# A two-layer diffusion trunk on one core: weight tiles of the modulation vectors loaded one step ahead of their dots, a fifth raw tile, and wider steps for the first layer's S5 tables

## The chip, the cores and the metric

One Trainium2 chip, one core. The metric is the device time of one execution in microseconds. The kernel before took 1841.99 us (median of 3 runs, 1840.18 to 1842.88).

## The reference, cut to what matters

The trunk has two layers over 256 latent tokens and 256 context tokens of width 1024 (512 columns in all). A layer is a SwiGLU half-step, a mixing sub-layer (windowed attention, a bidirectional S5 state-space part and a short gated convolution) and a second SwiGLU half-step. Each of the three sub-layers normalizes its input, shifts and scales it, and gates its output, with nine modulation vectors per layer that are products of a conditioning vector with a 1024 x 9216 matrix:

```python
def _modulate(x, g, shift, scale):
    return _rms_norm(x, g) * (1 + scale) + shift

def _gated_post(y, g, gate):
    return gate * _rms_norm(y, g)

def _swiglu(h, wg, wu, wd):
    return (jax.nn.silu(h @ wg) * (h @ wu)) @ wd

def _ffn_sublayer(x, m, s, g_pre, g_post, wg, wu, wd):
    h = _modulate(x, g_pre, m[:, 3 * s], m[:, 3 * s + 1])
    return _gated_post(_swiglu(h, wg, wu, wd), g_post, m[:, 3 * s + 2])
```

All is float32. The vectors are made for two conditioning inputs (latent and context tokens), so each weight tile of them is read by two dots.

## The kernel before, in words

**Products.** A float32 weight tile of 128 x 1024 comes from DRAM into a *raw* tile `wr` (`wraw`, L122), is rounded to `wh` by ACT (L131), and the rest `wl` is taken by POOL or DVE (L134). Activations are split the same way into `xh` (ACT, L608) and `xl` (DVE, L609), and a product is three matmuls, `wh` with the high part, `wh` with the low part and `wl` with the high part (`mm3`, L146; the matmuls are on L156). There are four raw tiles. They serve every such weight, the weights of the modulation vectors and a few scratch tiles of the S5 part.

**Stages.** FFN(0,0) is the first half-step of layer 0, then come the mixer of layer 0, FFN(0,1), FFN(1,0), the mixer of layer 1 and the last half-step. A half-step has 22 blocks of 128 hidden columns in four groups of 5, 5, 5 and 7: for each block the gate and up products (`pgu`), then the gate (`g`, ACT L606) times up (L607 on DVE, in place in `pgu`) and its split (L608, L609); after a group the down products (`pd`), which go through its blocks for one part of the output after the other, so that the first part needs all five blocks; L655 adds it into `y`. A half-step's first two column spans are run at 256 columns (`sk`), because the norm of the sub-layer ahead is still being formed for the second span.

**The boundary between sub-layers** (`boundary`, L372). For each of eight parts `d`, DVE makes `ss` (L381) and adds it into the stream `x` (L383); ACT squares it, PE sums the columns (`ss`, L341), DVE forms 1/sqrt in some ten small operations (L295 to L325) and puts it on a diagonal `dg` (L329), PE spreads it over the partitions (`rb`, L334), and DVE and ACT make the normalized input (`hh`, `hl`, L364 to L367).

**Side work.** Two kinds of side work run as generators beside the products: `ada` (L272) forms one modulation vector from eight tiles of 128 x 1024 of `w_ada`, each with two dots on DVE (L249; only one for the last vectors of layer 1); `ssm_tables` (L838) forms the S5 part's tables for a layer. A generator yields a number of ticks, and `mm3` counts ticks per matmul (1 tick is 2370 columns of matmul). When enough have passed, the generator's next piece is written into the program. So the tables `DTA` (per half-step, 5.1, 7.0 and 6.64 ticks per tile of `w_ada`) and `YS` (per piece of the S5 tables) say where in PE's order the pieces stand. The order of PE is fixed by this. The orders of DVE, ACT, POOL and SP come from a scheduler that works with its own times, and raw tiles are given to whichever load comes next in that order.

**The S5 tables of layer 0** are made in FFN(0,0) in four quarters. In a quarter POOL forms `tx` and `tvv` (L904, L907), PE transposes `tx` (`wt`, L914) after `YS[l][4]` ticks, twice, and after `YS[l][5]` makes `kp` (L934), which DVE finishes (`tz`, L939). `wt` and `kp` share two PSUM tiles. After the fourth quarter POOL makes the rotations (L956 to L978), and only behind those stand its `wl` splits for the last group's down weights.

**Queues.** SP issues every load and waits in order: a load that waits for its raw tile holds up those behind it, the loads `ts` of the S5 tables (L853 to L856) among them.

Of the kernel before, what the change touches and what calls it, by code (L numbers as in the profile page):

```python
# [8 lines left out]
F32 = mybir.dt.float32  # L9
# [12 lines left out]
KD = 8  # L22
# [8 lines left out]
FGROUPS = (tuple(range(0, 5)), tuple(range(5, 10)), tuple(range(10, 15)), tuple(range(15, 22)))  # L31
RF = -27.0 / 1024
MAGIC_ROUND = 12582912.0
RAW = 4
WB = 6
FIRST = 3
SKEW_IN = 4
# [31 lines left out]
DTA = (5.1, 7.0, 6.64)  # L69
YB = (2.2, 2.43, 9.63)  # L70
YP = (45.0, 8.0, 4.12, 5.43, 8.37, 8.88, 12.75)
YS = ((6.42, 1.34, 4.28, 18.82, 6.31, 3.09, 0.29, 3.43, 7.65), (6.0, 2.0, 4.0, 16.0, 16.0, 4.0, 2.0, 4.0, 8.0))
YA = (1.0, 5.0, 0.1)
ND = 3
NDL = 2
# [3 lines left out]
class Trunk:  # L79
# [42 lines left out]
    def wraw(self, src, cols=1024):  # L122
        w = self.wpool.tile([128, 1024], F32, name=self.nm("wr"), tag="wr", bufs=RAW)
        self.nc.sync.dma_start(w[:, :cols], src)
        return w
# [147 lines left out]
    def ada(self, l, m, dt):  # L273
        first = 1 if l == NL - 1 and m >= 5 else 0
        if first:
            self.nc.gpsimd.memset(self.mod[l][:, m], 0.0)
        for b in range(KD):
            w = self.wraw(self.a["w_ada"][l, m, b])
            for s in range(first, 2):
                self.ada_dot(w, l, m, b, s)  # L280
            yield dt
        self.ada_end(l, m, slice(0, KD))
        yield 0.1

# [121 lines left out]
    def rows(self):  # L406

        nc = self.nc
        l = NL - 1
        for i in range(2):  # L410
            p = self.pm("pr")
            nc.tensor.matmul(p[:KD, :128], self.pv[l][i + 1][:, :, 1], self.ident, start=True, stop=True)
            t = self.slots.tile([128, 512], F32, name=self.nm("bt"), tag="bt", bufs=2)[:KD, :128]
            nc.scalar.activation(t, p[:KD, :128], AF.Copy)
            dr = self.dram.tile([KD, 128], F32, name=self.nm("pvr"))
            nc.sync.dma_start(dr, t)
            nc.sync.dma_start(self.sb[:, i], dr.rearrange("d p -> (d p)")[None, :].to_broadcast([128, D]))
            yield

        self.xr = []  # L420
        for t in range(2):
            self.xr.append([])
            for h in range(2):
                p = self.pm("pxr")
                for d in range(4):
                    c = CTX + t * 128
                    nc.tensor.transpose(p[:, d * 128:d * 128 + 128], self.x[4 * h + d][:, c:c + 128], self.ident)
                d = 4 * t + 2 * h
                x = self.xall[:, d:d + 2, :256]
                p = p.rearrange("p (a b) -> p a b", a=2)  # L430
                if h:
                    nc.vector.tensor_copy(x, p)
                else:
                    nc.scalar.activation(x, p, AF.Copy)
                self.xr[t].append(x)
                yield
# [296 lines left out]
    def ssm_params(self):  # L733
# [25 lines left out]

        pw = self.wpool.tile([128, 1024], F32, name=self.nm("pw"), tag="wr", bufs=RAW)[:, :2 * 9 * w]  # L760
        pw = pw.rearrange("p (i k w) -> p i k w", i=2, k=9)
# [76 lines left out]
    def ssm_tables(self, l):  # L838
# [19 lines left out]
        par = [self.gg[:, :, l * 16:l * 16 + 16], self.u8[:, :, l * 16:l * 16 + 16], self.m8[:, l * 16:l * 16 + 16]]  # L858
        yield YS[l][0]
        b, c, pws, pr = tb("tvv", 2), tb("tc"), tb("tpw"), self.tpr  # L860
        for s_, d_ in zip(src, (b, c, pws)):
# [5 lines left out]
            else:  # L867
                nc.scalar.activation(d_, p, AF.Copy)
            yield YS[l][1]
        p = self.pm("tp")  # L870
        for s_, o, n in zip(par, (0, 32, 64), (32, 32, 16)):
            nc.tensor.matmul(p[:, o:o + n], self.ident, s_, start=o == 0, stop=True, skip_group_check=True)
        nc.scalar.activation(pr, p[:, :80], AF.Copy)
        yield YS[l][2]
        gg_, u8_ = (pr[:, o:o + 32].rearrange("p (i g) -> p i g", i=2) for o in (0, 32))
# [10 lines left out]
        for i, (x, y, o) in enumerate(((0, 1, OP.subtract), (1, 0, OP.add))):  # L886
# [3 lines left out]
            g.tensor_tensor(bbv[i][:, :, :16], tv[:, 0], tv[:, 1], op=o)  # L890
        yield YS[l][3]
        zd = self.dram.tile([256, 240], F32, name=self.nm("Z"))
        for gq in range(4):
# [3 lines left out]
            for ri in range(2):  # L897
# [12 lines left out]
                VV.append(vv)  # L910
                yield YS[l][4]
                pt = self.pm("wt")
# [6 lines left out]
                nc.sync.dma_start(self.V[l, gq // 2, ri][:, o], vv)  # L919
            yield YS[l][5]  # L920
            kp = self.pm("kp"), self.ps("kp")
# [63 lines left out]
    def ssm_chunks1(self, u):  # L985
# [3 lines left out]
        for half in range(2):  # L989
            t = self.wpool.tile([128, 1024], F32, name=self.nm("ut"), tag="wr", bufs=RAW)  # L990
            for jh in range(2):
# [77 lines left out]
    def ssm_out(self, l, gh, U, S, lo):  # L1069
# [6 lines left out]
        vt = [self.wraw(self.V[l, gh, ri]) for ri in range(2)]  # L1076
        yt = self.wpool.tile([128, 1024], F32, name=self.nm("yt"), tag="wr", bufs=RAW)
        ng, r = 128 // n, 8 * n // 128
# [139 lines left out]
    def mixer(self, l, H, pend, newH):  # L1218
# [143 lines left out]
        def early_out(n):  # L1362
# [10 lines left out]
            v=lambda n: vtok(), k=lambda n: ksplit(), q=qsplit,  # L1373
            s=lambda n: S.append(self.ssm_states(l, n, U)), o=lambda n: yt.append(self.ssm_out(l, n, U, S[n], lo)),
            b=lambda n: G.append(self.ssm_back(yt[n], lo)), w=weight, r=lambda n: next(rows, None),
            g=lambda n: self.ssm_glu(l, G, cat, lo), e=early_out, x=tail if last else bound, S=attn_s,
            y=lambda n: oevac(n // 10, n % 10), z=lambda n: self.advance(out[0][1]), W=weight,
# [19 lines left out]
    def first(self, H, ws):  # L1397
# [9 lines left out]
        nc.scalar.activation(self.cv, self.cv, AF.Silu)  # L1407
        nc.vector.tensor_copy(cv[:, :, :2], self.cv)
        rows, xn = {}, {}

        def row(d, *ms):
# [211 lines left out]
```

## Time and profile before

| | |
|---|---|
| median of 3 runs | 1841.99 us |
| profiled execution | 1845.4 us, span of the core 1843.1 us, 2.3 us around it |
| mean granted clock of TensorE | 0.968 |
| PE busy | 1724.7 us (94%) |
| DVE busy | 1139.7 us (62%) |
| POOL busy | 711.7 us (39%) |
| ACT busy | 657.8 us (36%) |

Busy time of PE counts a slow matmul as busy, so its share says little of how much is lost; what is lost shows as idle time ahead of a matmul and as a granted clock of 0.5, at which a matmul takes twice as long. A bracket behind an instruction is the idle time of its engine just before it, and what ended it.

### The profile page before, as it was taken

To read this page: it belongs to the slowest core of one execution; us is meant where nothing else is said; L and a number is where in the kernel's file an instruction comes from. 1 tells how busy PE (TensorE), PEld (TensorE's weight loads), DVE (VectorE), ACT (ScalarE), POOL (GpSimd) and SP (SyncE) were. 2 spreads that over 40 slices of the span, in tenths; PEclk is the share of its full clock that TensorE was granted. 3 is DMA by queue.
4 is the path that set the end of the run, shared out by engine and by line. 5 is a ranking of instruction groups with operands and counts; after the bars stand their busy time and mean duration, and the time that the engine had idled before them with its cause. 6 is when DMAs were issued, how large, how long until landed. Compare 5 with 4: busy or idle time off the path is not lost.

```text
span 1843.1 us, 28602 instructions
## 1 busy us (share of the span) xinstructions
PE 1724.7 (94%) x11040; PEld 1483.2 (80%) x11040; DVE 1139.7 (62%) x2228; ACT 657.8 (36%) x1173; POOL 711.7 (39%) x623
## 2 busy tenths in 40 slices
PE   7999988998987989999999989999999899889998
PEld 5887876898975879887888989888888897679997
DVE  5798786726479655787774265765456466852223
ACT  4332222324334543322222243322222344445443
POOL 4100886854344142563438343000001553435552
PEclk9999998999999988999999999999999989899999
DMA  7666556644144021665655331646466424445662
GB/s 279 227 221 179 183 175 185 212 137 127 35 143 142 26 82 43 197 193 180 194 189 166 96 115 55 227 147 200 126 205 221 128 93 140 145 151 174 191 184 92
DMA packets 103481, 285.94 MB, mean 155 GB/s; under 512 B 19904, under 2 KB 27152, under 8 KB 103344
## 3 DMA queue, kind: packets, MB, share of 16 engines
q1 hardware_dynamic: 102992, 283.91, 49.1%
q8 instruction: 87, 1.43, 0.3%
q14 instruction: 50, 0.41, 0.1%
q0 software_dynamic: 64, 0.12, 0.0%
q10 hardware_dynamic: 288, 0.07, 0.0%
HBM read 270.45 MB, written 15.70 MB: 155 GB/s over the span
## 4 chain that ended last, share of the span: by engine, by line
PE 71%; DVE 13%; DMA 6%; issue 4%; POOL 3%; ACT 3%; SPq 0%; DVEq 0%; ACTq 0%; POOLq 0%
PE pgu L156 32%; PE pd L156 17%; PE sk L156 8%; PE yr L484 4%; DMA wr<-in_w_ada_dram 3%; DVE junk L249 3%; PE po L156 2%; DVE wl L134 2%; PE ss L341 1%; ACT wh L131 1%; DMA wr<-in_w_in_dram 1%; PE pgu L535 1%; PE O L1209 1%; DVE xacc L354 1%; DVE ss L381 1%
## 5 line engine op out<-in xcount | busy, mean ns | idle before, releaser
L134 POOL TENSOR_TENSOR wl<-wr,wh 128x1024 fp32r<-128x1024 f32 (+1 forms) x140 | 326.1, 2345 | 704.7 <-ACT wh L131 314.1
L131 ACT ACTIVATE wh<-wr 128x1024 fp32r<-128x1024 f32 (+2 forms) x350 | 341.8, 983 | 636.3 <-PE pgu L156 164.9
L156 PE MATMUL pgu<-hh,wh 128*128 128x512 f32 (+1 forms) x1296 | 469.8, 363 | 0.0
L156 PE MATMUL pgu<-hl,wh 128*128 128x512 f32 (+1 forms) x1296 | 465.2, 359 | 0.0
L156 PE MATMUL pgu<-hh,wl 128*128 128x512 f32 (+1 forms) x1296 | 465.2, 359 | 0.0
L249 DVE SCALAR_TENSOR_TENSOR junk<-wr,sb 128x1024 bf16<-128x1024 f32 x224 | 311.9, 1392 | 164.9 <-DMA wr<-in_w_ada_dram 163.2
L134 DVE TENSOR_TENSOR wl<-wr,wh 128x1024 fp32r<-128x1024 f32 (+1 forms) x210 | 251.4, 1199 | 70.0 <-ACT wh L131 69.2
L156 PEld LDWEIGHTS pgu<-hh,wh 128*128 128x128 f32 x1296 | 244.6, 189 | 41.1 <-issue 1.7
L156 PEld LDWEIGHTS pgu<-hl,wh 128*128 128x128 f32 x1296 | 244.6, 189 | 39.8 <-issue 0.5
L156 PEld LDWEIGHTS pgu<-hh,wl 128*128 128x128 f32 x1296 | 244.3, 189 | 39.2
L156 PE MATMUL pd<-xh,wh 128*128 128x512 f32 (+1 forms) x696 | 245.6, 353 | 7.6 <-ACT xh L608 7.6
L156 PE MATMUL pd<-xl,wh 128*128 128x512 f32 (+1 forms) x696 | 241.6, 347 | 1.1 <-DVE xl L609 1.1
L156 PE MATMUL pd<-xh,wl 128*128 128x512 f32 (+1 forms) x696 | 240.6, 346 | 0.0
L156 PEld LDWEIGHTS pd<-xh,wh 128*128 128x128 f32 x696 | 135.0, 194 | 25.9 <-ACT xh L608 8.9
L156 PEld LDWEIGHTS pd<-xl,wh 128*128 128x128 f32 x696 | 134.8, 194 | 19.6 <-DVE xl L609 2.8
L156 PEld LDWEIGHTS pd<-xh,wl 128*128 128x128 f32 x696 | 134.7, 194 | 16.2
L156 PE MATMUL sk<-hh,wh 128*128 128x256 f32 x480 | 141.6, 295 | 0.0
L156 PE MATMUL sk<-hl,wh 128*128 128x256 f32 x480 | 139.1, 290 | 0.1
L156 PE MATMUL sk<-hh,wl 128*128 128x256 f32 x480 | 138.8, 289 | 0.0
L608 ACT ACTIVATE xh<-pgu 128x512 fp32r<-128x512 f32 (+1 forms) x61 | 35.0, 574 | 175.5 <-DVE pgu L607 175.3
L156 PEld LDWEIGHTS sk<-hl,wh 128*128 128x128 f32 x480 | 94.7, 197 | 0.6 <-DVE hl L367 0.3
L156 PEld LDWEIGHTS sk<-hh,wh 128*128 128x128 f32 x480 | 94.7, 197 | 0.3
(375 smaller groups left out, 2479.4 us busy)
## 6 DMA issues: line engine op xcount, KB each, us to landing
wr<-in_wgu_dram SPq DMA_DIRECT2D x170, 512.0 KB, 4.3
wr<-in_w_ada_dram SPq DMA_DIRECT2D x144, 512.0 KB, 4.3
wr<-in_wd_dram SPq DMA_DIRECT2D x72, 320.0 KB, 3.2
wr<-in_w_in_dram SPq DMA_DIRECT2D x32, 512.0 KB, 3.9
wr<-in_wd_dram SPq DMA_DIRECT2D x36, 448.0 KB, 3.8
wr<-in_wdr_dram SPq DMA_DIRECT2D x22, 512.0 KB, 3.6
wr<-in_w_out_dram SPq DMA_DIRECT2D x10, 512.0 KB, 5.0
V<-tvv SPq DMA_DIRECT2D x16, 256.0 KB, 2.8
```

Of the source, the lines that this page charges most:

```text
L131: nc.scalar.activation(h[:, :cols], w[:, :cols], AF.Copy)
L134: eng.tensor_tensor(lo[:, :cols], w[:, :cols], h.bitcast(F32)[:, :cols], op=OP.subtract)
L156: mm = lambda a_, x_, st, sp: nc.tensor.matmul(po, a_[:, c], x_[:, lo:hi], start=st, stop=sp, skip_group_check=True)
L249: self.nc.vector.scalar_tensor_tensor(self.junk, w, 1.0, self.sb[:, s], op0=OP.mult, op1=OP.mult, accum_out=self.mod[l][:, m, b, s:s + 1])
L341: self.nc.tensor.matmul(p[:, b:b + 1], t[:, lo + b * 128:lo + (b + 1) * 128], self.ones[:, 0:1], start=first and b == 0, stop=last, skip_g ...
L354: nc.vector.tensor_tensor(acc[:, lo:hi], acc[:, lo:hi], sq, op=OP.add)
L381: nc.vector.scalar_tensor_tensor(bt, y[d][:, lo:hi], self.pv[l][s_][:, d, s:s + 1], rb[:, :hi - lo], op0=OP.mult, op1=OP.mult)
L484: mm = lambda x_, a_, st, sp: self.nc.tensor.matmul(p, x_[:, c], a_[:, o:o + 512], start=st, stop=sp, skip_group_check=True)
L535: nc.tensor.matmul(ps[i // 2][:, o:o + 128], w[:, k * 128:k * 128 + 128], U[k][:, t * 128:t * 128 + 128], start=t + n + i % 2 == 0, stop=n ...
L608: nc.scalar.activation(gh[:, lo:hi], pu, AF.Copy)
L1209: nc.tensor.matmul(O[pr, :w], vt[:, kt * 128 + 64 * ab:kt * 128 + 64 * ab + 64], PT[ab][:, kt * w:(kt + 1) * w], start=kt == 0, stop=kt == ...
```

## The change

There are five edits. A fifth raw tile (`RAW`). In `ada`, the load of tile b + 1 is written one step before the dots of that tile, so that a load has a whole step (5.1 to 7.0 ticks) before its dots; the loads stand at the same ticks as before and the dots one step later. In the first layer's S5 tables, `YS[0][4]` goes from 6.31 to 8.3 and `YS[0][5]` from 3.09 to 4.0, so that a quarter takes 2 x 8.3 + 4.0 + 0.29 = 20.89 ticks in place of 16.00. In `rows`, two small tiles move to the common pool of 39, which frees the room for the fifth raw tile. All lines behind L280 stand five lines lower in the changed kernel.

```diff
-RAW = 4
+RAW = 5
-YS = ((6.42, 1.34, 4.28, 18.82, 6.31, 3.09, 0.29, 3.43, 7.65), (6.0, 2.0, 4.0, 16.0, 16.0, 4.0, 2.0, 4.0, 8.0))
+YS = ((6.42, 1.34, 4.28, 18.82, 8.3, 4.0, 0.29, 3.43, 7.65), (6.0, 2.0, 4.0, 16.0, 16.0, 4.0, 2.0, 4.0, 8.0))
...
+        load = lambda b: self.wraw(self.a["w_ada"][l, m, b])
+        ws = [load(0)]
+        yield dt
         for b in range(KD):
-            w = self.wraw(self.a["w_ada"][l, m, b])
+            if b < KD - 1:
+                ws.append(load(b + 1))
             for s in range(first, 2):
-                self.ada_dot(w, l, m, b, s)
-            yield dt
+                self.ada_dot(ws[b], l, m, b, s)
+            if b < KD - 1:
+                yield dt
         self.ada_end(l, m, slice(0, KD))
         yield 0.1
...
-            t = self.slots.tile([128, 512], F32, name=self.nm("bt"), tag="bt", bufs=2)[:KD, :128]
+            t = self.slot("pvt")[:KD, :128]
```

**How the order moves, 1: DVE at the boundary ahead of FFN(0,1).** These are the last of the eight parts and the start of the 1/sqrt. Before:

```order
L381 SCALAR_TENSOR_TENSOR ss_6766<-y_4810,pv_105,rb_6818 128x256
L383 TENSOR_TENSOR x<-x,ss_6766 128x256
L607 TENSOR_TENSOR sk_6743<-g_6905,sk_6743 128x256
L295 TENSOR_SCALAR v_6974<-ss_6969 128x2
L609 TENSOR_TENSOR xl_6904<-sk_6743,xh_6903 128x256
```

In the changed kernel, with the rest of the 1/sqrt:

```order
L386 SCALAR_TENSOR_TENSOR ss_6766<-y_4810,pv_105,rb_6818 128x256
L249 SCALAR_TENSOR_TENSOR junk,mod_96<-wr_7352,sb 128x1024
L388 TENSOR_TENSOR x<-x,ss_6766 128x256
L249 SCALAR_TENSOR_TENSOR junk,mod_96<-wr_7352,sb 128x1024
L612 TENSOR_TENSOR sk_6743<-g_6905,sk_6743 128x256
L300 TENSOR_SCALAR v_6974<-ss_6969 128x2
```

```order
L330 TENSOR_SCALAR r_6980<-rd_6983,ri_6976 128x1 x2
L249 SCALAR_TENSOR_TENSOR junk,mod_96<-wr_7416,sb 128x1024
L323 TENSOR_SCALAR t_6988<-r_6980,v_6974 128x1 x2
L249 SCALAR_TENSOR_TENSOR junk,mod_96<-wr_7416,sb 128x1024
L330 TENSOR_SCALAR r_6989<-t_6988,r_6980 128x1 x2
L334 TENSOR_SCALAR dg_6994<-ident,r_6989 128x128 x2
```

The four dots of the first two tiles of this half-step, which stood behind all of the boundary's work, now stand inside its chain. The same four stand at the same places of the chain ahead of FFN(1,0).

**How the order moves, 2: SP at the same place.** The loads from the last gate and up weights ahead of FFN(0,1)'s first tile of `w_ada` on; the name behind "waits" is the engine whose reading frees the raw tile. In the changed kernel:

```order
L124 DMA wr_7341<-in_wgu_dram 128x1024 [waits DMAHW0_49,Pool_49]
L124 DMA wr_7352<-in_w_ada_dram 128x1024 [waits DMAHW1_49,Pool_49]
L124 DMA wr_7416<-in_w_ada_dram 128x1024 [waits DMAHW6_49,DVE_49]
L124 DMA wr_7451<-in_wd_dram 128x640 [waits DMAHW7_49,DVE_49]
```

The raw tile that `wr_7352` takes is the one of `wr_7019`, from which POOL makes the second of two `wl`; the kernel before loads `wr_7341` at that point. The tile that `wr_7416` takes is that of `wr_7352`: it waits for both dots of it.

**How the order moves, 3: DVE at the end of the third group of FFN(0,0)**, from the fourth block's product (`pgu_2226`; `pgu_2247` before) to the fifth's. Before:

```order
L249 SCALAR_TENSOR_TENSOR junk,mod_96<-wr_2698,sb 128x1024
L940 SCALAR_TENSOR_TENSOR tz_2341<-mask_715,ssmd,tz_2341 128x16
L607 TENSOR_TENSOR pgu_2247<-g_2368,pgu_2247 128x512
L134 TENSOR_TENSOR wl_2614<-wr_2610,wh_2612 128x640
L609 TENSOR_TENSOR xl_2367<-pgu_2247,xh_2366 128x512
L134 TENSOR_TENSOR wl_2656<-wr_2652,wh_2654 128x640
L607 TENSOR_TENSOR pgu_2386<-g_2466,pgu_2386 128x512
```

In the changed kernel:

```order
L612 TENSOR_TENSOR pgu_2226<-g_2304,pgu_2226 128x512
L134 TENSOR_TENSOR wl_2550<-wr_2546,wh_2548 128x640
L614 TENSOR_TENSOR xl_2303<-pgu_2226,xh_2302 128x512
L249 SCALAR_TENSOR_TENSOR junk,mod_96<-wr_2721,sb 128x1024 x2
L134 TENSOR_TENSOR wl_2573<-wr_2569,wh_2571 128x640
L944 TENSOR_TENSOR tz_2418<-tz_2418,kp_2384 128x16
L945 SCALAR_TENSOR_TENSOR tz_2418<-mask_715,ssmd,tz_2418 128x16
L612 TENSOR_TENSOR pgu_2322<-g_2445,pgu_2322 128x512
```

Two dots now stand between the two products, and the load of their tile `wr_2721` takes the raw tile that `wl_2550` reads, so it is issued behind that row.

## Rows read from the trace of the kernel before

**Rows 1.** The chain that ended last: shares by engine; a run of matmuls (start, us).
```profile
PE 71%; DVE 13%; DMA 6%; issue 4%; POOL 3%; ACT 3%; SPq 0%; DVEq 0%; ACTq 0%; POOLq 0%
...
1189.78 56.00 PE pgu L156 x240
```

**Rows 2.** Timeline of PE: four stops (start us, us, instruction, idle before).
```profile
178.14 0.79 PE L156 MATMUL pd<-xh,wh 128*128 128x512 f32 x1 [3.30 <-ACT xh L608]
...
258.64 0.45 PE L914 MATMUL wt<-ident,tx 128*128 128x128 f32 x1 [5.66 <-DVE tz L939]
...
286.58 1.09 PE L914 MATMUL wt<-ident,tx 128*128 128x128 f32 x4 [5.69 <-DVE tz L939]
...
855.96 0.50 PE L156 MATMUL pd<-xh,wh 128*128 128x512 f32 x1 [2.94 <-ACT xh L608]
```

**Rows 3.** Windows: busy us of PE, PEld, DVE, ACT, POOL; granted clock, DMA share, GB/s.
```profile
206.00:262.00 56.00, 50.34 (x278) 40.67 (x277) 49.14 (x52) 12.17 (x18) 55.06 (x37) 0.94 0.54 173
...
257.00:262.00 5.00, 3.36 (x10) 2.90 (x11) 4.33 (x8) 0.34 (x1) 4.84 (x3) 0.50 0.63 206
...
711.00:716.50 5.50, 5.50 (x26) 5.50 (x27) 3.99 (x20) 2.33 (x7) 0.00 (x0) 0.50 0.00 0
```

**Rows 4.** Windows of the dots alone: busy us of DVE and ACT, then the clock.
```profile
62.00:138.00 76.00, 39.80 (x62) 0.00 (x0) 1.00 0.66 209
206.00:262.00 56.00, 31.94 (x35) 0.00 (x0) 0.94 0.54 173
```

**Rows 5.** Timeline of DVE, second and third groups of FFN(0,0).
```profile
191.21 0.69 DVE L655 TENSOR_TENSOR y<-y,pd 128x512 f32<-128x512 f32 x1 [6.04 <-PE pd L156]
...
285.12 1.22 DVE L249 SCALAR_TENSOR_TENSOR junk<-wr,sb 128x1024 bf16<-128x1024 f32 x1 [4.40 <-DMA wr<-in_w_ada_dram]
...
290.79 0.68 DVE L607 TENSOR_TENSOR pgu<-g,pgu 128x512 f32<-128x512 f32 x1
```

**Rows 6.** Timeline of DVE, FFN(0,1).
```profile
850.51 1.27 DVE L249 SCALAR_TENSOR_TENSOR junk<-wr,sb 128x1024 bf16<-128x1024 f32 x1 [4.93 <-DMA wr<-in_w_ada_dram]
```

**Rows 7.** Timeline of POOL at the boundary ahead of FFN(0,1); the page's DMA issues (KB, us to landing).
```profile
702.24 4.75 POOL L134 TENSOR_TENSOR wl<-wr,wh 128x1024 fp32r<-128x1024 f32 x2 [12.81 <-PE sk L156]
...
wr<-in_w_ada_dram SPq DMA_DIRECT2D x144, 512.0 KB, 4.3
```

**Rows 8.** Timelines of DVE and PE at the boundary ahead of FFN(0,1).
```profile
709.45 0.42 DVE L383 TENSOR_TENSOR x<-x,ss 128x256 f32<-128x256 f32 x1
...
715.65 0.28 DVE L329 TENSOR_SCALAR dg<-ident,r 128x128 f32<-128x128 f32 x1
...
710.38 1.02 PE L341 MATMUL ss<-ones,xsq 128*128 128x1 f32 x4
...
716.51 0.59 PE L334 MATMUL rb<-dg,ones 128*128 128x256 f32 x2
```

**Rows 9.** Timelines of POOL and DVE at the boundary ahead of FFN(1,0).
```profile
1110.23 4.74 POOL L134 TENSOR_TENSOR wl<-wr,wh 128x1024 fp32r<-128x1024 f32 x2 [9.47 <-PE sk L156]
...
1117.45 0.42 DVE L383 TENSOR_TENSOR x<-x,ss 128x256 f32<-128x256 f32 x1
...
1122.22 0.28 DVE L329 TENSOR_SCALAR dg<-ident,r 128x128 f32<-128x128 f32 x1
```

**Rows 10.** The chain in order of time: a load of w_in in the second mixer.
```profile
1548.26 6.84 DMA wr<-in_w_in_dram
```

**Rows 11.** Timelines of POOL and PE: the rotations, the next splits, the last group's down products.
```profile
311.91 0.11 POOL L957 MEMSET tx<- 128x8 f32 x1 [5.20 <-PE wt L914]
...
383.36 2.14 POOL L134 TENSOR_TENSOR wl<-wr,wh 128x896 fp32r<-128x896 f32 x1 [5.89 <-ACT wh L131]
...
393.21 0.28 PE L156 MATMUL pd<-xh,wh 128*128 128x256 f32 x1
```

**Rows 12.** Timelines of SP and PE in FFN(0,1): the S5 table loads, and the transposes that read them.
```profile
744.85 0.42 SPq L853 DMA_DIRECT2D ts<-in_ssm_b_dram  x1
...
751.31 0.59 PE L863 MATMUL tp<-ts,ident 128*128 128x512 f32 x1
```

## The prediction

> **What bounds the kernel now.** I read the page's chain first: PE holds 71% of it, DVE 13% and DMA 6% [rows 1]. So most of the time is matmuls that nothing can move, and what a change of loads and side work can win is the time in which PE stands. I then went through PE's timeline for stops inside the half-steps, away from the boundaries. There are four large ones [rows 2]: A at 178.14 (3.30 us, for the split `xh` of a down product), B at 258.64 and C at 286.58 (5.66 and 5.69 us, `wt` waiting until DVE's `tz` has freed a PSUM tile) and D at 855.96 (2.94 us, again `xh`). After such a stop the matmuls run at a granted clock of 0.50 for a while: the window behind B holds 3.36 us of matmuls at 0.50 [rows 3], of which half, 1.7 us, is lost. I add 1.7 us to each stop: A 5.0, B 7.4, C 7.4, D 4.6; A to C make 19.8.
>
> Who is late there is read from DVE's own timeline. At C it waits 4.40 us for a tile of `w_ada` directly before `tz`, and the gate products queue behind it: the last block's product of the third group runs at 290.79 [rows 5]. At D a dot waits 4.93 us for its tile [rows 6]. DVE is also slowed: a dot with its read-out takes 39.80 / 31 = 1.28 us in the window 62 to 138, and 31.94 over some 17.5 dots = 1.82 us between 206 and 262, where POOL is busy for 55.06 of 56 us with the S5 tables [rows 3, 4].
>
> **The change, part by part.**
>
> *Stops A to C in FFN(0,0).* The wider steps move `wt` and `kp` back by up to 4 x 4.89 ticks; a tick is 2370 columns and a matmul of 512 takes 56.00 / 240 = 0.233 us [rows 1], so 1.08 us a tick and 21 us in all. So `tz` is no longer what C or B waits for. But the down products of the third group need the fifth block's product from DVE, which came at 290.79, after `tz`. Without the wait for `wt` PE would need it some 20 us earlier, and DVE has to have done the same dots and splits by then. So I cost A to C by DVE's arrival there, from `y` at 191.21 on: (1) the second group's down products start their first part earlier by what A gives back. DVE's gate products there now stand ahead of the dots, but SP's loads `ts` of the tables stand behind three more raw loads, one of which waits for the group's last `wl`; I expect a short stop for them in place of the long one, and take 3.5 of A's 5.0. (2) The two dots that used to follow `y` now run in the 6.04 us in which DVE waited for it [rows 5]: 2.5. (3) DVE loses to POOL about (1.82 - 1.28) / 1.82 of its 49.14 busy us between 206 and 262, 14.6, and some 18 in the whole stretch; the quarters are now 20.89 ticks long and not 16.00, so POOL does 0.77 of the table work in it: 4.1 less. (4) The waits for `w_ada`: per tile, landing time 4.3 [rows 7] less the DVE work that the new order has between the row that frees the raw tile and the dot. For the last four tiles of the stretch that work is one or two small operations, so nearly the whole landing shows; over the stretch the sum is 17.8 us by the new order and 14.2 by the old. The fifth tile doesn't shorten them, since the scheduler hands it on at once. Zero is my value, as the early tiles' waits vanish. Sum: 3.5 + 2.5 + 4.1 = 10.1, I take **-10**. Ends: -2 (nothing but part of A) and -19.8 (all).
>
> *Stop D in FFN(0,1).* The boundary below brings PE there some 6 us later, with two tiles' dots already done, and DVE is 3 us late now: **-4.6**, ends 0 and -4.6.
>
> *The boundaries ahead of FFN(0,1) and FFN(1,0).* This is the added wait. Four dots, two tiles, now stand inside DVE's chain of the boundary. The first tile can't be issued before POOL's second `wl` of the pair is done, at 702.24 + 4.75 = 706.99, and lands 4.3 later [rows 7], at 711.3. DVE comes to the dot before the last `x`, which ran at 709.45 [rows 8]. It waits to 711.3, works 1.28, and `x` runs at 712.6: +3.1. ACT's square and PE's sum (710.38) follow it. The tile's second dot is done by 714.2; only then is the second tile issued, landing at 718.5, where 1/sqrt has long been ready for its last step. Two dots and the step between them take it to 721.3, and `dg` runs at 721.7 in place of 715.65. PE's `rb` at 716.51 had 0.4 us to spare: **+5.6**. Ahead of FFN(1,0) [rows 9] POOL ends at 1114.97, the tile lands at 1119.3, `x` comes at 1120.5 in place of 1117.45, the second tile lands at 1126.5, and `dg` runs at 1129.7 in place of 1122.22; with 0.6 us to spare, **+6.9**. Queued behind these dots on DVE are `dg`, all of the normalized input and the gate products; PE has matmuls of the first span for the time ahead of `rb`, and they are already counted. Each stop may bring a stretch at half clock, 1.7 as above; the matmuls ahead of `rb` run at 0.50 already [rows 3], so I take 1 each, +2. Together **+14.5**. Lower end: tiles that land in time leave x + 1.28 and two dots in 1/sqrt, 3.8 each, 7.6. Upper end: 12.5 + 3.4 + 2 for slower landings, 18.
>
> *Loads `ts` in FFN(0,1).* Before, they were issued at 744.85 and read by `tp` at 751.31 [rows 12]. Now five more raw loads stand ahead, but PE comes 5.6 later too. So an issue up to 5.6 us later is hidden as before, and the cover is gone where SP comes to them later than at 750.5; a whole landing of 4.3 is the upper end, zero stands in the sum.
>
> *The rotations.* They begin when the last `wt` is done (311.91) and end 65.6 us later, 5.89 before 383.36; PE wanted the split behind them at 393.21, so there were 7.7 us to spare [rows 11]. Now that `wt` runs at 311.91 + 21 - 10 = 323, PE wants the split at 383.4, and at the same pace it would be ready at 390.7. But a rotation step is slow only beside DVE's dots, which end at about the same time as before less the gain: +1, ends 0 and +7.
>
> *Mixers.* One more weight tile can be in flight. The chain has a load of `w_in` with 6.84 us in the second mixer [rows 10]; a load that starts one tile earlier can save part of that until attention binds: **-2**, ends 0 and -5. The tiles moved to the common pool cost nothing, they are two copies of 8 x 128.
>
> **Sum:** -10 - 4.6 + 14.5 + 1 - 2 = **-1.1 us** against the profiled execution's 1845.4, which is 3.4 above the median; on the median, **1841 us**. About 0.2% (3.7 us) is what a measurement of this kernel can tell from no change. The forecast's own range, with A to C from -5 to -15 and the boundaries from 11 to 17, is 1834 to 1849.
>
> The weakest term is (3). The row shows slower dots beside POOL, not which operation blocks which. The Trainium skill, SBUF — State Buffer, section "Summary: rules for kernel authors", says that when a DVE operation with two SBUF inputs meets a GpSimd operation that reads SBUF, the second one to issue "fully blocks until the first finishes". By that, a busy DVE meets a POOL operation as often as POOL runs any, whatever the pitch, and DVE's loss per quarter stays; the trace's 1.82 against 1.28 fits it. By that rule term (3) would be zero and the sum +3.0, 1845; it is half of rival 2, and there its chance is.
>
> **Rivals.**
>
> 1. *DVE catches up* (faster). If the loads, written a step ahead, land before their dots, DVE is in time and A to C go whole: -19.8 in place of -10, sum -10.9, 1831. For it: the waits of 4.40 and 4.93 are just such loads [rows 5, 6], and the four table quarters spread over 21 us more of PE's time. Against it: the order frees raw tiles right before the dots. Should the boundaries also cost only 7.6, it is 1824.
>
> 2. *DVE stays as late as before* (slower). Place: the fifth block's product of the third group, at 290.79. With 3.6 us more of waits (17.8 against 14.2) and without the 4.1 that less POOL work gives, DVE arrives 10.1 - 3.6 - 4.1 = 2.4 us earlier than before, and the boundaries are paid in full: sum +6.5, 1848.5. It decides against the kernel once A to C return less than 5.2. For it: the new order has two dots, and a load behind the row just ahead, between the fourth and fifth blocks. Against it: the earlier waits of the stretch vanish in the order.
>
> 3. *Nothing moves*: the scheduler's orders on DVE give the same waits at other places and the boundaries hide them behind the first span's matmuls; 1842. Against it: `rb` has 0.4 us to spare.
>
> **How the numbers follow.** Forecast 0.50, of which 0.15 is faster by over 0.2%, 0.29 within and 0.06 slower; rival 1 0.23 (faster); rival 2 0.21 (slower); rival 3 0.06 (same). So faster 0.38, same 0.35, slower 0.27. The range, 1827 to 1851, takes rival 1 down to a bit over half of its way to 1824, and rival 2 with 3 us for slower landings or the rotations; outside lie the whole gain with cheap boundaries and several upper ends together.
>
> **What would show it.** Right: dots with waits of 2 and 4 us between the last `x` and `dg` at about 710 and 1118, and `rb` about 6 us later against the `x` before; no stop before `wt` in FFN(0,0), but one of 5 us or more in the third group's down products for `xh`; no stop like D. Wrong: a third group without a stop (rival 1), a stop there as late as before (rival 2), or dots in the boundary that don't wait. A new stop before the last group's down products, or at `tp`, would be the terms that I set near zero.

## Result, and the profile after

The changed kernel takes **1855.51 us** (median of 4 runs, 1854.22 to 1861.99) against 1841.09 for the kernel before (4 runs, 1838.62 to 1842.88): ratio 1.0086, 95% interval 1.0059 to 1.0113. It is slower, and outside the forecast range of 1827 to 1851. The profiled execution took 1856.31 us with a span of 1854.5.

PE's timeline of the changed kernel, for the stops of [rows 2] (start us, us, instruction, idle before and its releaser):

```profile
178.81 0.80 PE L156 MATMUL pd<-xh,wh 128*128 128x512 f32 x1 [4.14 <-ACT xh L613]
...
277.95 0.79 PE L156 MATMUL pd<-xh,wh 128*128 128x512 f32 x1 [4.52 <-ACT xh L613]
...
289.25 0.50 PE L156 MATMUL pd<-xh,wh 128*128 128x512 f32 x1 [0.91 <-ACT xh L613]
290.86 0.50 PE L156 MATMUL pd<-xl,wh 128*128 128x512 f32 x1 [1.11 <-DVE xl L614]
...
702.64 0.61 PE L346 MATMUL ss<-ones,xacc 128*128 128x1 f32 x4 [2.65 <-DVE ss L386]
705.85 1.01 PE L346 MATMUL ss<-ones,xsq 128*128 128x1 f32 x4 [2.60 <-ACT xsq L356]
...
713.85 0.67 PE L339 MATMUL rb<-dg,ones 128*128 128x256 f32 x2 [2.04 <-DVE dg L334]
...
937.31 0.80 PE L156 MATMUL pd<-xh,wh 128*128 128x512 f32 x1 [3.88 <-ACT xh L613]
...
1122.01 1.01 PE L346 MATMUL ss<-ones,xsq 128*128 128x1 f32 x4 [2.65 <-ACT xsq L356]
...
1130.13 0.67 PE L339 MATMUL rb<-dg,ones 128*128 128x256 f32 x2 [2.03 <-DVE dg L334]
```

Stop A stays; B, C and D are gone. The third group's down products stop at 277.95 for the fourth block's `xh` and, for 0.91 and 1.11 us, at 289.25 and 290.86 for the fifth block's. New are the waits for `xsq` and for `dg` in the two boundaries (the one of 2.65 us for `xacc` stands in the kernel before too, at 709.47), and a stop at 937.31 that no part of the sum held.

DVE at the boundary ahead of FFN(0,1), the rows that answer to [rows 8]:

```profile
700.89 0.42 DVE L388 TENSOR_TENSOR x<-x,ss 128x256 f32<-128x256 f32 x1
...
703.78 1.23 DVE L249 SCALAR_TENSOR_TENSOR junk<-wr,sb 128x1024 bf16<-128x1024 f32 x1 [1.19 <-DMA wr<-in_w_ada_dram]
...
704.93 0.42 DVE L388 TENSOR_TENSOR x<-x,ss 128x256 f32<-128x256 f32 x1
705.26 1.22 DVE L249 SCALAR_TENSOR_TENSOR junk<-wr,sb 128x1024 bf16<-128x1024 f32 x1
...
710.33 1.22 DVE L249 SCALAR_TENSOR_TENSOR junk<-wr,sb 128x1024 bf16<-128x1024 f32 x1
...
711.84 1.22 DVE L249 SCALAR_TENSOR_TENSOR junk<-wr,sb 128x1024 bf16<-128x1024 f32 x1
...
713.22 0.48 DVE L334 TENSOR_SCALAR dg<-ident,r 128x128 f32<-128x128 f32 x2
```

and ahead of FFN(1,0), answering to [rows 9]:

```profile
1117.00 0.42 DVE L388 TENSOR_TENSOR x<-x,ss 128x256 f32<-128x256 f32 x1
...
1119.93 1.23 DVE L249 SCALAR_TENSOR_TENSOR junk<-wr,sb 128x1024 bf16<-128x1024 f32 x1 [1.24 <-DMA wr<-in_w_ada_dram]
...
1121.09 0.42 DVE L388 TENSOR_TENSOR x<-x,ss 128x256 f32<-128x256 f32 x1
...
1126.60 1.23 DVE L249 SCALAR_TENSOR_TENSOR junk<-wr,sb 128x1024 bf16<-128x1024 f32 x1 [1.15 <-DMA wr<-in_w_ada_dram]
...
1129.51 0.47 DVE L334 TENSOR_SCALAR dg<-ident,r 128x128 f32<-128x128 f32 x2
```

The first row of each is the seventh of the eight `x`; in the kernel before these are:

```profile
707.73 0.42 DVE L383 TENSOR_TENSOR x<-x,ss 128x256 f32<-128x256 f32 x1
```

```profile
1115.72 0.42 DVE L383 TENSOR_TENSOR x<-x,ss 128x256 f32<-128x256 f32 x1
```

From the last `x` to `dg` it is 713.22 - 704.93 = 8.29 us here, 6.20 before; ahead of FFN(1,0) 8.42 against 4.77. The delay of the last `x` itself by the first dot comes on top. The first tile's dot waits 1.19 and 1.24 us. The second tile's dot waits 1.15 us ahead of FFN(1,0) and not at all ahead of FFN(0,1), where the steps of 1/sqrt and the gate products keep DVE busy until it runs.

The new stop at 937.31 is read from DVE:

```profile
933.52 1.22 DVE L249 SCALAR_TENSOR_TENSOR junk<-wr,sb 128x1024 bf16<-128x1024 f32 x1 [4.65 <-DMA wr<-in_w_ada_dram]
...
934.78 1.22 DVE L249 SCALAR_TENSOR_TENSOR junk<-wr,sb 128x1024 bf16<-128x1024 f32 x1
...
935.93 0.69 DVE L612 TENSOR_TENSOR pgu<-g,pgu 128x512 f32<-128x512 f32 x1
```

and from SP's queue, which issues that load 5 us ahead of the dot:

```profile
928.54 0.33 SPq L124 DMA_DIRECT2D wr<-in_w_ada_dram  x1
```

DVE has nothing to do for 4.65 us, and the gate product that PE needs stands behind the two dots. In the kernel before, that product stood ahead of the waiting dot:

```profile
930.89 0.68 DVE L607 TENSOR_TENSOR pgu<-g,pgu 128x512 f32<-128x512 f32 x1
...
937.57 1.23 DVE L249 SCALAR_TENSOR_TENSOR junk<-wr,sb 128x1024 bf16<-128x1024 f32 x1 [3.98 <-DMA wr<-in_w_ada_dram]
```

Windows of the changed kernel behind the stop (columns as in [rows 3]) show what follows it:

```profile
937.31:944.00 6.69, 6.69 (x18) 5.02 (x19) 3.38 (x6) 2.53 (x5) 0.14 (x2) 0.55 0.93 286
944.00:950.00 6.00, 6.00 (x27) 4.89 (x26) 3.06 (x5) 2.60 (x4) 0.17 (x1) 1.00 0.33 92
```

There are 3.88 us of idle and then 6.69 us of matmuls at a mean granted clock of 0.55, of which 45%, 3.0 us, is lost: 6.9 of the 7.0 us by which the kernel falls back here.

**Stage by stage.** All kernels below run the same 8088 matmuls of the helper at L156, so the start of the k-th one can be set against that of the k-th one before. The table holds, for each stretch (times of the kernel before), how much longer it is than in the profile of before, in us; the total runs from the first to the last of these matmuls. Worked out from the traces:

```
                      157-394  394-639  639-725  836-863  863-972 1068-1138 1466-1688  total
                      FFN(0,0) mixer 0  to (0,1) stop D   (0,1)   to (1,0)  mixer 1
after                   -4.7     -0.5     +4.4     -4.7     +7.0     +7.3      +3.9    +11.3
load-ahead alone        -2.0     -1.1     +2.6     -0.1     +0.1     +2.7      +1.2     +1.8
wider steps alone       -1.0     -3.0     -0.5     -0.3     +0.1     +2.7      +1.1     -2.3
the same, once more     +0.7     -3.0     +2.5     -0.1     +0.1      0.0      +1.7     +1.9
common slots alone      -3.3     +0.8     -1.4     +1.0     +0.1     +0.4      +6.8     +3.8
fifth tile alone        +0.3     -0.9     +7.2     -4.9     +6.0     +8.4      +3.0    +17.7
after, no load-ahead    -4.3     +0.1     +5.2     -5.0     +7.0     +7.3      +5.8    +14.8
narrow dots             -6.4     -2.2     +3.8     -5.2     +6.7     +2.8      +6.9     +5.4
held loads              -7.4     -3.3     +2.5     -1.0      0.0     +0.1      +6.3     -3.1
no dots, after          -5.8     -3.4     +2.4     -5.1     +0.1     +0.3      +6.5     -5.3
no dots, before         -4.2     -1.4     +2.5     -5.1     +0.1     +1.5      +2.6     -4.8
rows in dots' output    -7.6     -1.8     +7.4     -4.7     +6.6     +7.2      +1.4     +7.9
held + rows there       -8.9     -0.9     -0.5     -0.8      0.0     -0.1      +2.5     -9.1
```

The second row is a caution: that kernel's instructions stand in exactly the order of before on all five engines, and yet a stage differs by up to 2.7 us. One profile prices a stage to some 3 us, no better; what is said of stages below rests on groups of rows.

### The profile page after: what moved, and what is told of

It reads as the page before. It is cut to its first block, busy times and chain, and to the rows that moved or that the text cites. A ratio compares the mean times of both kernels' runs of the same rounds, so it can differ in the third digit from the quotient of the medians.

```text
span 1854.5 us, 28617 instructions
## 1 busy us (share of the span) xinstructions
PE 1731.2 (93%) x11040; PEld 1489.7 (80%) x11040; DVE 1141.5 (62%) x2228; ACT 654.9 (35%) x1173; POOL 697.8 (38%) x623
## 5 line engine op out<-in xcount | busy, mean ns | idle before, releaser
L156 PE MATMUL pgu<-hh,wh 128*128 128x512 f32 (+1 forms) x1296 | 468.9, 362 | 0.0
L156 PE MATMUL pgu<-hl,wh 128*128 128x512 f32 (+1 forms) x1296 | 464.5, 358 | 0.2 <-DVE hl L1469 0.2
L156 PE MATMUL pgu<-hh,wl 128*128 128x512 f32 (+1 forms) x1296 | 464.3, 358 | 0.0
L156 PEld LDWEIGHTS pgu<-hh,wh 128*128 128x128 f32 x1296 | 244.1, 188 | 40.1 <-issue 1.7
L156 PEld LDWEIGHTS pgu<-hl,wh 128*128 128x128 f32 x1296 | 244.2, 188 | 39.5 <-DVE hl L1469 0.5
L156 PEld LDWEIGHTS pgu<-hh,wl 128*128 128x128 f32 x1296 | 244.2, 188 | 38.6
L156 PE MATMUL pd<-xh,wh 128*128 128x512 f32 (+1 forms) x696 | 246.9, 355 | 13.5 <-ACT xh L613 13.5
L156 PE MATMUL pd<-xl,wh 128*128 128x512 f32 (+1 forms) x696 | 243.2, 349 | 1.7 <-DVE xl L614 1.7
L156 PE MATMUL pd<-xh,wl 128*128 128x512 f32 (+1 forms) x696 | 242.1, 348 | 0.0
L156 PEld LDWEIGHTS pd<-xh,wh 128*128 128x128 f32 x696 | 135.8, 195 | 31.7 <-ACT xh L613 15.0
L156 PEld LDWEIGHTS pd<-xl,wh 128*128 128x128 f32 x696 | 135.8, 195 | 20.4 <-DVE xl L614 3.8
L156 PEld LDWEIGHTS pd<-xh,wl 128*128 128x128 f32 x696 | 135.9, 195 | 16.2
L156 PE MATMUL sk<-hh,wh 128*128 128x256 f32 x480 | 142.9, 298 | 0.0
L156 PE MATMUL sk<-hl,wh 128*128 128x256 f32 x480 | 140.4, 292 | 0.5 <-DVE hl L372 0.5
L156 PE MATMUL sk<-hh,wl 128*128 128x256 f32 x480 | 140.1, 292 | 0.0
L156 PEld LDWEIGHTS sk<-hl,wh 128*128 128x128 f32 x480 | 96.0, 200 | 1.0 <-DVE hl L372 0.7
L156 PEld LDWEIGHTS sk<-hh,wh 128*128 128x128 f32 x480 | 96.1, 200 | 0.2
```

Source lines behind the costliest of these rows:

```text
L156: mm = lambda a_, x_, st, sp: nc.tensor.matmul(po, a_[:, c], x_[:, lo:hi], start=st, stop=sp, skip_group_check=True)
```

## Experiments

Theory F: the fifth raw tile, through the order that the scheduler gives DVE, carries the loss. The rivals: L, the loads that run ahead; W, T, G, M as the expectations name them. Theory S says that the two moved tiles, not the fifth raw tile, make mixer 1 longer.

**1. The load-ahead edit alone** (four raw tiles, old steps).

```diff
+        load = lambda b: self.wraw(self.a["w_ada"][l, m, b])
+        ws = [load(0)]
+        yield dt
         for b in range(KD):
-            w = self.wraw(self.a["w_ada"][l, m, b])
+            if b < KD - 1:
+                ws.append(load(b + 1))
```

> The kernel before with the load-ahead edit alone (four raw tiles, old widths). Theory F (the fifth tile carries the cost; the order that the scheduler gives the dots follows from when their data is there by its own reckoning, not from the step in which they are written): nothing moves on any engine, 1841 us, within 0.2%, and the four stops at 178, 259, 287 and 856 us stand as before. Rival L (the loads that run ahead are what puts the dots among the boundaries and ahead of the gate products): 1848 us or more, with new stops near 703, 933 and 1119 us.

1844.74 us (10 runs) against 1843.48: ratio 1.0007 [0.9994, 1.002]. Every row stands where it stood on all five engines. Where a dot is written in `ada` does not decide its place on DVE; the raw tiles do.

**2. The wider steps alone**, twice.

```diff
-YS = ((6.42, 1.34, 4.28, 18.82, 6.31, 3.09, ...
+YS = ((6.42, 1.34, 4.28, 18.82, 8.3, 4.0, ...
```

> The kernel before with the two wider steps of the first layer's S5 tables alone. Theory F: FFN(0,0) gains about what the changed kernel gained there, 5 us, and all the rest stands still: the stop at 856 us (4.6 us) stays, the boundaries ahead of FFN(0,1) and FFN(1,0) keep their lengths; 1834 to 1838 us. Rival W (the gain in FFN(0,0) comes from the fifth tile): 1839 to 1843 us, with the stops at 259 and 287 us still there.

1847.04 us (12 runs), 1.0024 [1.0011, 1.0037]. Neither theory had this. Its profile fell on its fastest run, so it ran once more:

> The kernel with the wider steps alone once more, for a second profile: its first one fell on the fastest of its runs. If the wider steps alone cost time, this profile shows FFN(0,0) longer than in the kernel before, or a stop elsewhere, and 1846 to 1848 us; if the first result was the spread of single runs, 1841 to 1844 us, with FFN(0,0) shorter than before by 1 to 5 us.

1847.89 us (10 runs) against 1843.08, 1.0023 [1.0013, 1.0034]: a small loss, shown twice. FFN(0,0) reads -1.0 and +0.7, where the four kernels of the old steps and four tiles (the kernel before, and those with load-ahead, with common slots and without dots) read 0, -2.0, -3.3 and -4.2. DVE of the second profile says why:

```profile
281.61 2.15 DVE L249 SCALAR_TENSOR_TENSOR junk<-wr,sb 128x1024 bf16<-128x1024 f32 x1 [2.59 <-DMA wr<-in_w_ada_dram]
...
283.69 0.68 DVE L609 TENSOR_TENSOR xl<-pgu,xh 128x512 fp32r<-128x512 f32 x1
```

and PE, at the third group's down products:

```profile
278.67 0.80 PE L156 MATMUL pd<-xh,wh 128*128 128x512 f32 x1 [3.73 <-ACT xh L608]
284.42 0.79 PE L156 MATMUL pd<-xl,wh 128*128 128x512 f32 x1 [4.95 <-DVE xl L609]
...
296.01 0.50 PE L156 MATMUL pd<-xh,wh 128*128 128x512 f32 x1 [3.53 <-ACT xh L608]
```

Stops B and C go, and three stops for gate products take their place, each behind a dot that waits for its tile. Cut at three of the helper's matmuls, FFN(0,0) takes (us, from the traces):

```
                          535th to 941st   to 1001st   to 1425th   sum
before                        116.7          25.9         94.3     236.9
wider steps alone (2nd)       104.5          36.1         97.1     237.6
after                         106.7          28.0         97.4     232.2
```

Up to the third group the wider steps win 10 to 12 us with either number of tiles; the third group takes 10.2 of them back with four tiles and 2.1 with five, and another 3 go behind it (1.4 of these is `wt` and `kp` work that has only moved there).

**3. The fifth tile alone** (with the two small tiles moved, which make the room).

```diff
-RAW = 4
+RAW = 5
-            t = self.slots.tile([128, 512], F32, name=self.nm("bt"), tag="bt", bufs=2)[:KD, :128]
+            t = self.slot("pvt")[:KD, :128]
```

> The kernel before with the fifth raw tile alone (and the small tile that pays for it in memory), loads not ahead, old widths. Theory F: all the cost of the changed kernel and none of the gain of the wider steps: both boundaries longer by 4 to 7 us each, a new stop of 4 us in the second half of FFN(0,1), mixer 1 about 3 us longer, the stop at 856 us gone (-4.7): 1856 to 1863 us. Rival L: below 1846 us. Rival W: like the changed kernel or a little above it, 1854 to 1857 us, with FFN(0,0) already shorter.

1862.91 us (4 runs), 1.0107 [1.0085, 1.0128], 19 us above the kernel before, with both boundaries longer, the stop in FFN(0,1) and stop D gone, as theory F has it. Kernel 4 below has the wider steps besides and takes 8 us less (1854.92), with -4.3 in FFN(0,0) where this one reads +0.3: with five tiles the wider steps do help, and rival W falls.

**4. The changed kernel without the load-ahead edit.** The diff is that of 1 taken back.

> The changed kernel without the load-ahead edit. Theory F: the same instructions in the same order, so the same time, 1855 us, within 0.2%. Rival L: at least 5 us below the changed kernel, 1850 us or less.

1854.92 us (4 runs), 1.0066 [1.0042, 1.009]: the changed kernel's time, from the same rows in the same order. Rival L falls.

**5. The first loads of (0,8) and (1,3) held back**, which takes the dots out of the two boundaries.

```diff
+HOLD = 30.0
+        if (l, m) in ((0, 8), (1, 3)):
+            yield HOLD
```

> The changed kernel with the first load of tile (0,8) and of tile (1,3) held back by 30 ticks: no dot stands any longer between the last x and dg of the two boundaries. Theory F (dots that stand in the boundary chains, put there by the fifth tile, make 11 to 13 us of the loss): both boundaries return to the lengths of before (4 to 6 us and 7 us less), the stop in the second half of FFN(0,1) stays or moves: 1842 to 1846 us. Rival T (the boundaries are longer because more transfers run beside them with five tiles): the boundaries keep their length, 1852 to 1857 us.

1846.13 us (10 runs), 1.0008 [0.9993, 1.0024]. The boundaries return to what four-tile kernels show. The stop in FFN(0,1)'s second half goes too, since all later dots move with the first; so does most of the gain at D's place (-1.0 in the table, where the changed kernel has -4.7): a dot waits ahead of a gate product there again. Of rival T, what more transfers beside the boundary would cost, the other loads are ruled out, since the fifth tile is still there; the held loads themselves have left the boundaries with their dots, and experiment 6 keeps them.

**6. Narrow dots in the boundaries.**

```diff
+        n = 16 if (l, m) in ((0, 8), (1, 3)) and b < 2 else D
-        ...scalar_tensor_tensor(self.junk, w, 1.0, self.sb[:, s], ...
+        ...scalar_tensor_tensor(self.junk[:, :n], w[:, :n], 1.0, self.sb[:, s, :n], ...
```

> The changed kernel with the dots of the first two tiles of (0,8) and of (1,3), the four that stand in each boundary, cut from 1024 columns to 16: same loads, same places. What is left out: most of those two parts of the modulation. Theory F, if it is the dots' own time that counts: 4 x 1.1 us less in each boundary, 1846 to 1848 us. Rival G (the wait for the landing of the load counts, and a shorter dot is made up by a longer wait): each boundary loses less than 2.2 us, 1851 us or more.

1850.76 us (9 runs), 1.0047 [1.0031, 1.0064], between the two. The loads stand where they stood; the second tile's dots have moved a few steps forward in the 1/sqrt. Ahead of FFN(1,0) DVE shows:

```profile
1115.13 0.17 DVE L250 SCALAR_TENSOR_TENSOR junk<-wr,sb 128x16 bf16<-128x16 f32 x1 [1.23 <-DMA wr<-in_w_ada_dram]
...
1119.43 0.18 DVE L250 SCALAR_TENSOR_TENSOR junk<-wr,sb 128x16 bf16<-128x16 f32 x1 [1.27 <-DMA wr<-in_w_ada_dram]
...
1121.44 0.47 DVE L335 TENSOR_SCALAR dg<-ident,r 128x128 f32<-128x128 f32 x2
```

The waits are those of the full dots (1.23 and 1.27, against 1.24 and 1.15): a shorter dot is not made up by a longer wait, so G falls. From the last `x` (1115.23) to `dg` it is 6.21 us, 2.2 less than with full dots, and the last `x` comes 1 us sooner behind that wait. In the table the two boundaries read +6.6 together, where the four kernels with full dots in them read 13.5 and the six with four raw tiles 2.2. So some 6.9 of 11.4 us go with the dots' own time. The waits for the landing, which are all still there, are what the rest is put down to; it was not shown by itself.

**7 and 8. No dots of (0,8) and the second layer**, in the changed kernel and in the kernel before.

```diff
+        if (l, m) == (0, 8) or l == 1:
+            self.nc.vector.memset(self.mod[l][:, m], 0.0)
+            yield dt
+            self.ada_end(l, m, slice(0, KD))
+            return
```

> The changed kernel without the dots of (0,8) and of the whole second layer, and without their loads (those parts of the modulation are left out and set to zero). Theory F: boundaries (11 to 13 us) and the stop at 933 us (4 to 7 us) go, FFN(0,0) and its gain are untouched: 1834 to 1839 us. Rival T (the fifth tile costs by the weights' own loads and by where it puts the wl work): 1846 us or more.

> The kernel before without the same dots and loads (set to zero): what the dots cost there. Theory F: they stand in no boundary there, only the stop at 856 us goes: 1836 to 1839 us. If the dots cost more than the stops show (slowing of GpSimd beside them, traffic), 1830 us or less.

1841.99 us, 0.9993 [0.9979, 1.0007], and 1838.71 us, 0.9972 [0.9957, 0.9987] (10 runs each). In the kernel before these dots cost 5 us, as much as stop D reads in the table (-5.1). In the changed kernel they cost 15 us (1.0076, the mean of the two kernels of the same order, less 0.9993), net of stop D, which is gone there in either case. Without dots the changed kernel is still 3 us above its counterpart, and its table row shows where: mixer 1, +6.5 against +2.6.

**9 and 10. Mixer 1.** The changed kernel differs there by its orders, though no dots run. The kernel before with the two small tiles moved to the common slots, and nothing else, already has on DVE a `gelu` product, which waits for ScalarE, ahead of a copy of PT. So that edit ran alone, and then the changed kernel with those tiles put elsewhere:

```diff
-            t = self.slots.tile([128, 512], F32, name=self.nm("bt"), tag="bt", bufs=2)[:KD, :128]
+            t = self.slot("pvt")[:KD, :128]
```

> The kernel before with one edit alone: the two small tiles of pv's rows in mixer 1 are taken from the 39 common slots instead of a place of their own (in the change this pays for the fifth tile); four raw tiles, old widths, loads not ahead. Theory S (this edit, not the fifth tile, makes mixer 1 longer: the scheduler then puts a gelu product that waits for ScalarE ahead of a copy of PT on VectorE): 3 to 5 us above the kernel before, all of it between 1580 and 1650 us, 1847 to 1849 us beside 1843.7. Rival M (mixer 1 is longer because of the fifth tile's earlier weight loads): the same as before within 0.1%, mixer 1 included.

```diff
-            t = self.slot("pvt")[:KD, :128]
+            t = self.junk.bitcast(F32)[:KD, i * 128:i * 128 + 128]
```

> The changed kernel with the rows of pv written into the dots' idle output tile instead of common slots: five raw tiles stay, the order on VectorE at the end of mixer 1 is that of before again (copy of PT ahead of the gelu product). Theory S: mixer 1 returns to within 2 us of before, 3 to 5 us less than the changed kernel: 1850 to 1853 us. Rival M: mixer 1 stays 4 us or more longer, 1855 us.

The first: 1848.47 us (8 runs), 1.0026 [1.0013, 1.004], mixer 1 +6.8. DVE in its mixer 1:

```profile
1606.89 0.69 DVE L1109 TENSOR_SCALAR gelu<-gelu 128x256 f32<-128x256 f32 x1 [1.82 <-ACT gelu L1108]
1607.50 0.68 DVE L1196 COPY PT<-pt 128x512 f32<-128x512 f32 x1
```

The changed kernel has the same wait, of 1.76:

```profile
1614.27 0.77 DVE L1114 TENSOR_SCALAR gelu<-gelu 128x256 f32<-128x256 f32 x1 [1.76 <-ACT gelu L1113]
1614.96 0.68 DVE L1201 COPY PT<-pt 128x512 f32<-128x512 f32 x1
```

and with the tiles in the dots' output the copy stands ahead again:

```profile
1607.41 0.69 DVE L1201 COPY PT<-pt 128x512 f32<-128x512 f32 x1 [0.26 <-PE pt L1198]
1609.14 0.34 DVE L1114 TENSOR_SCALAR gelu<-gelu 128x256 f32<-128x256 f32 x1 [1.03 <-ACT gelu L1113]
```

Mixer 1 reads +3.0 to +6.9 in the seven kernels with the common slots, with four raw tiles or five, and 0 to +2.6 in the seven without. Rival M falls. The total of this second kernel, 1854.81 us (4 runs, 1.0063 [1.0048, 1.0078]), is a miss: mixer 1 gave 2.5 us, the boundaries in this profile took 2.8 more than in that of the changed kernel. By the ratios (1.0063 against 1.0076) it is 2.4 us below the changed kernel, which the intervals cannot tell from nothing. That the one swap makes all of mixer 1's 4 us is read from the timelines, not shown by itself; other rows of DVE move there too.

**11. Both cures together**, 5 and the second of 9 and 10.

> The version that the runs so far point to: the changed kernel, first loads of (0,8) and (1,3) held back by 30 ticks (no dots in the boundaries), and pv's rows in the dots' idle output tile (mixer 1 ordered as before). By theory F and S together, from the run with the held loads (1846.1) less 4 us in mixer 1: 1841 to 1843 us, 0.1% below the kernel before; by rival M, 1845 to 1847 us.

1842.79 us (12 runs) against 1843.08, 0.9991 [0.9979, 1.0004]: as forecast, 16 us below the changed kernel by the ratios (1.0076, the mean of its two kernels of one order, less 0.9991), and not to be told from the kernel before. Its profile fell on the fastest of its runs, 1835.7, so its table row is a good one. It keeps the gain in FFN(0,0) and has lost that at D. No version here is clearly faster than the kernel before, save that kernel itself without its dots.

## Why the prediction was wrong

The sum was -1.1; in its place stands +14 (1.0076 of 1842; 11.3 in the profile). Its terms, each as the mean of the kernels that have the mechanism less the mean of those that don't:

- **The boundaries, +14.5: right in the path, 3 too much.** Measured +11.4 (13.5 in the four kernels with full dots there, 2.2 in the six with four raw tiles). The first tile lands 1.2 us after DVE asks for it, where the working had 1.9; `x` is late by this wait and a dot, and the second tile's two dots stand inside the 1/sqrt. The second wait is what I had wrong. I took 1/sqrt for ready long before the second tile landed, and named a wait of 4 us as a sign; but its steps have DVE until about the landing, so that the wait is 0 and 1.15 us. `dg` came 4.4 and 6.0 us later against the seventh `x`, where +6.05 and +7.5 was the working.
- **Stop D, -4.6: right.** -5.0.
- **A to C, -10: right in its sign, mis-sized.** Measured -4.1 (-6.4 in seven kernels, -2.4 in the four of the old order). The step that failed is DVE's arrival at the fifth block's product of the third group, which was to be 10.1 us earlier than 290.79. It came at 287.87, 2.9 earlier, since between the fourth block's product, 11.1 us earlier than before, and this one DVE waits 4.44 us for the tile of the two dots that now stand there:

```profile
276.58 0.68 DVE L612 TENSOR_TENSOR pgu<-g,pgu 128x512 f32<-128x512 f32 x1
...
283.50 2.10 DVE L249 SCALAR_TENSOR_TENSOR junk<-wr,sb 128x1024 bf16<-128x1024 f32 x1 [4.44 <-DMA wr<-in_w_ada_dram]
...
287.87 0.69 DVE L612 TENSOR_TENSOR pgu<-g,pgu 128x512 f32<-128x512 f32 x1
```

  In the seven kernels with both edits the fifth product comes 1.3 to 4.5 us earlier, counted from the 535th matmul (2.7 in the changed kernel), and in the four of the old order 0 to 5.1. Nor did PE's gain hang on this arrival alone. In the kernel before, the fifth block had been split (292.82) some 6 us before PE came to it:

```profile
298.96 0.39 PE L156 MATMUL pd<-xh,wh 128*128 128x512 f32 x1
```

  In the changed kernel PE comes to it 9.7 us sooner, at 289.25, and now does wait there. From the 941st matmul on, 5.2 of the 10 us won ahead of it are lost again (the small table above), for which I had priced nothing. Term (3), 4.1 us less of slowing by POOL, has no row to stand on: between 206 and 262 a dot takes 34.62 / 19 = 1.82 us in the changed kernel as well, and POOL is busy for 52.24 of 56 us, not for 0.77 of the 55.06 before:

```profile
206.00:262.00 56.00, 56.00 (x309) 45.45 (x308) 53.53 (x58) 11.35 (x17) 52.24 (x32) 1.00 0.57 176
```

```profile
206.00:262.00 56.00, 34.62 (x38) 1.00 0.57 176
```

  (The first row is of all engines, the second of the dots alone.) The wider pitch did not thin POOL's work there. By the rule that the prediction weighed, from the section "Summary: rules for kernel authors" of the Trainium skill's page SBUF — State Buffer, the term would be zero, and the trace agrees: 1.82 us in both kernels. Terms (1) and (2) were together 6.0. Stop A was not shortened in this profile (4.14 against 3.30), so how the 4.1 that came divide between them is open.
- **A new stop in FFN(0,1), not in the sum: +6.6.** Under *Stop D* I asked whether dots would still be late there, and took "two tiles' dots already done" for the whole half-step. What is late next I didn't ask: with the fifth tile the dots move up by one place all along FFN(0,1), at 933.52 ahead of a gate product instead of behind it. It appears in all five five-tile kernels that have these dots at their early places, and in no other.
- **"The tiles moved to the common pool cost nothing": wrong, +4.1.** I priced the two copies and not what the other slots do to the order. Of *Mixers, -2*, nothing shows: no gain from the fifth tile in mixer 1.
- **Rotations and `ts`, +1 and 0: no cost shows.** POOL starts the split behind the rotations at 380.10, before 383.36; PE's transposes of `ts` run at 750.23 with no stop near them. One reading there was wrong: a rotation step is slow not only beside dots. Of the 35 steps of 128x8 in the kernel before that took 0.8 to 1.3 us in place of 0.20, 13 ran beside a `wl` split on DVE and no dot.

-4.1 - 5.0 + 11.4 + 6.6 + 4.1 make 13.0 of the 14; mixer 0 shows no clear difference. The sign of the sum hung on A to C, the unpriced stop and the moved tiles: with what they measured in place, -1.1 becomes -1.1 + 5.9 + 6.6 + 4.1 = +15.5, and the other terms as measured (boundaries 3.1 less, D 0.4 more, no +1 for the rotations and no -2 for the mixers) bring that to the 13.0. Rival 2 had the side, the place and DVE's arrival there (2.4 us earlier), less than 5.2 back from A to C and the boundaries in full, at 1848.5; it lacked the stop in FFN(0,1) and mixer 1, 10.7 together, where 7.0 were missing.

The section on the change says that dots stand one step later. That is so in the program as written; in the order that runs, the edit moves nothing.

## What to carry to other kernels

A larger pool of buffers is not only room: the order on every engine is made from when buffers are free, so price each place where the order moves, also far from the loads, and ask at each what now stands behind a wait. Work that waits for a transfer should stand behind the products that the bounding engine needs, not ahead of them. And run the same instructions twice before one profile's stage is believed: here two profiles of one order differed by 2.7 us in a stage.

## What was not expected of the hardware

- A 4.65 us wait on DVE cost 7.0 us of PE's time: after 3.88 us of idle the next 6.69 us of matmuls ran at a mean granted clock of 0.55, so 3.0 us were lost behind the stop, where the prediction added 1.7 to each.
- A wider pitch of GpSimd's table work hardly made VectorE's dots beside it quicker: between 206 and 262 us a dot took 1.62 to 1.82 us in the nine kernels with the wider steps and 1.71 to 1.82 in the five without, against 1.28 where GpSimd is busy for 5.49 of 76 us. GpSimd still filled 89 to 95% of that window, against 94 to 98%.
- The time of one order spreads over more than 10 us: 1837.31 to 1848.61 us in 23 runs of the kernel before, with a mean granted clock of 0.971 in the fastest and 0.963 in the slowest.
